# Output projection of a two-layer decoder trunk: half of its first-half products moved from attention to the projection stage

## The chip, the cores and the metric

The kernel runs on one core of a Trainium2 chip. TensorE (PE) multiplies, with its weight loads beside it (PEld); VectorE (DVE), ScalarE (ACT) and GpSimd (POOL) do elementwise work; SyncE (SP) issues all DMAs, in order. The metric is the device time of one execution in microseconds, as a median over runs.

## The reference

Two residual layers on x of 1024 tokens by 1024 features, float32. Layer 0 mixes with 8 forgetting-attention heads and 8 latent-attention (MLA) heads, layer 1 with 8 differential heads; both map the concatenated heads back by one output projection. A gated MLP with a causal convolution follows. What matters here:

```python
for layer in range(DEPTH):
    h = _rms_norm(x, norm_mix_pre[layer])
    m = mixer(h)                               # ends in: heads @ w_out
    x = x + _rms_norm(m, norm_mix_post[layer])
    h = _rms_norm(x, norm_ffn_pre[layer])
    f = _conv_ffn(h, ffn_w_up[layer], ...)
    x = x + _rms_norm(f, norm_ffn_post[layer])
```

## The kernel before, in words

Every float32 operand of a product is split into a high part, cast to the type float32r, and the low remainder; a product is three matmuls, high by high, high by low, low by high (mm3, L139). A split is a cast on ACT and a subtraction on POOL or DVE (L119).

Attention of a layer runs head by head as a generator. Beside it runs a second generator, "dense": the projections of later heads, and last out_first (L446), the first half of the output projection. weave (L286) takes steps of dense between the steps of a head, as much as a table entry for that head allows (MLA_DENSE L40, DIFF_DENSE L29, in units of 2400 columns, about a microsecond). A scheduler then sets each engine's order from dependences and its own estimate of times; each engine works its list in order.

The heads' outputs, transposed, go to DRAM as oT: 8 tiles of 128 features, in high and low parts. The output projection multiplies them, for each of 8 tiles of 128 tokens (m, from 7 down to 0), with w_out in two column halves of 512 (n). The features are taken in two groups of four, kg 0 and kg 1. In layer 0 group 0 are the forgetting heads and group 1 the MLA heads; in layer 1 group 0 are heads 0 to 3. So group 0 is ready while the later heads still run:

- out_first multiplies group 0 for both column halves, 8 x 2 x 12 = 192 matmuls per layer, and copies each sum on ACT (L459) to SBUF tiles opart.
- out_second (L462), after attention, multiplies group 1, again 192 matmuls, into a bank of tag S (n = 0) or mm (n = 1), adds opart on DVE (L479), and runs the two norms: fin_e after the first half (square on ACT L202, times gain on POOL L203), fin_a after the second (square L212, POOL's multiply L213, the row's scale by rstd_col L153, x updated on DVE L216 and L217, stored L219; then pre_norm_a: square L225, scale, xn L227). fin_b of the tile before transposes xn on PE (L235) and evacuates it as operands of the up-projection (ffn_in_evac L492; B, T1f, T2f, T4f).
- From tile 3 on the first two feature tiles of the up-projection are prepared (prep L551: weights wg, wv, their splits S3, S4, A11, A12, S1, S2, A22 in tiles of tag Q) and two of their products are run ahead (run_a L587).

Buffers with a part in this: Q 18 tiles of 128x512 (keys and queries of heads, then weights of the projection's first half, then prep's splits), WL 8 (loads of oT, named ot), X 14 quads, T 6 (x and xn of a token tile), raw 2, and in PSUM 2 banks of tag S and 2 of mm. In layer 1 a differential head ends in sub_a and sub_b (L1138, L1155): a square, a sum over features on PE (L1146), Newton steps on DVE, then the store to oT.

Of the kernel before, what the change touches and what calls it, by code (L numbers as in the profile page):

```python
# [19 lines left out]
P = 128  # L20
# [5 lines left out]
NP = 11  # L26
TAIL = 5
FOX_DENSE = (21, 21, 16, 16, 21, 21, 5, 13)
DIFF_DENSE = (29, 31, 28, 32, 30, 30, 28, 25)  # L29
GRAIN = 1  # L30
LAG = 8
NA = 2
# [4 lines left out]
VT = "Q"  # L37
SB = 4
P2T = "mm"
MLA_DENSE = (8, 8, 6, 6, 6, 7, 18, 18)  # L40
HALF = 512
EPS = 1e-6
BIG = 3.0e38
# [18 lines left out]
def trunk(ctx: ExitStack, tc: tile.TileContext, a: dict):  # L62
# [13 lines left out]
    def buf(tag, name):  # L76
        return sb.tile(SHAPE[tag], F32, tag=tag, name=nm(name), bufs=BUFS[tag])
# [3 lines left out]
    def bank(tag, n=HALF):  # L81
        return ps.tile([P, n], F32, tag=tag, name=nm("ps" + tag), bufs=PB[tag])
# [120 lines left out]
        nc.gpsimd.tensor_tensor(src, src, g_post[n], ALU.mult)  # L203
        return ss

    def post_late(m, n, src, sse, early, g_post, xi, xq, cut=False):


        xr, xn = xq
        cs, ce = (slice(i * HALF, (i + 1) * HALF) for i in (n, 1 - n))  # L210
        ss = small(1, "ssl")
        nc.scalar.activation(xn[:, cs], src, AF.Square, accum_out=ss)  # L212
        nc.gpsimd.tensor_tensor(src, src, g_post[n], ALU.mult)  # L213
        nc.vector.tensor_scalar(ss, ss, sse, None, ALU.add)
        r = rstd_col(ss, 1.0 / D, "post")
        nc.vector.scalar_tensor_tensor(xr[:, ce], early, r, xr[:, ce], ALU.mult, ALU.add)  # L216
        nc.vector.scalar_tensor_tensor(xr[:, cs], src, r, xr[:, cs], ALU.mult, ALU.add)  # L217
        for c in (ce, cs) if cut else (slice(0, D),):
            nc.sync.dma_start(xd[xi + 1][m * P:(m + 1) * P, c], xr[:, c])  # L219
# [210 lines left out]
                res.append((hi, lo))  # L430
        return res

    def oT_load(oT, kg, m):
        ts = []
        for j in range(2):
            t = buf("WL", "ot")
            nc.sync.dma_start(t.rearrange("p (k c) -> p k c", k=4),
                              oT[j, 4 * kg:4 * kg + 4, :, m * P:(m + 1) * P].rearrange("k p c -> p k c"))
            ts.append(t)
        return ts  # L440

    def wo_quads(w_src, k0, n):
        q = [buf("X", "wo") for _ in range(2)]
        return wo_load(w_src, k0, n, lambda k: (q[0][:, k, :], q[1][:, k, :]))

    def out_first(w_src, oT, part):  # L446

        w = [wo_quads(w_src, 0, n) for n in range(2)]
        for m in range(7, -1, -1):
            ot = oT_load(oT, 0, m)  # L450
            for n in range(2):
                if (m // 4, n) not in part:
                    part[m // 4, n] = buf("X", "opart")
                o = bank("mm")
                for k in range(4):
                    mm3(o, hl(tuple(t[:, k * P:(k + 1) * P] for t in ot), w[n][k]), k == 0, k == 3)
                    if k < 3:
                        yield
                nc.scalar.copy(part[m // 4, n][:, m % 4, :], o)  # L459
                yield  # L460

    def out_second(w_src, oT, part, fin_0, fin_e, fin_a, fin_b, ahead):  # L462


        w = [wo_load(w_src, 4, 0, lambda k: (buf("Q", "woh"), buf("Q", "wol"))), wo_quads(w_src, 4, 1)]
        ot = {m: oT_load(oT, 1, m) for m in (7, 6, 5)}
        fin_0(7)
        for m in range(7, -1, -1):
            if m >= 3:
                ot[m - 3] = oT_load(oT, 1, m - 3)  # L470
            if m:
                fin_0(m - 1)
            rows = []
            for n in range(2):
                o = bank("S" if n == 0 else "mm")
                r = part[m // 4, n][:, m % 4, :]
                for k in range(4):
                    mm3(o, hl(tuple(t[:, k * P:(k + 1) * P] for t in ot[m]), w[n][k]), k == 0, k == 3)
                nc.vector.tensor_tensor(r, r, o, ALU.add)  # L479
                rows.append(r)  # L480
                if n == 0:
                    fin_e(m, 0, r)
            fin_a(m, 1, rows[1], rows[0])
            if m < 7:
                fin_b(m + 1)
            if m == 3:
                ahead(0)
        ahead(1)
        fin_b(0)
# [551 lines left out]
    def mixer_end(layer, w_src, oT, part):  # L1041
        B, xqs, sse = {}, {}, {}
        gpost = gain_post(a["g_mix_post"][layer])
        gpre = gain_bc(a["g_ffn_pre"][layer], buf("T", "gain"))

        def fin_0(m):
            xqs[m] = xq_pair("T")
            x_load(m, 2 * layer, xqs[m])

        def fin_e(m, n, src):  # L1050
            sse[m] = post_early(n, src, gpost, xqs[m][1][:, :HALF])

        def fin_a(m, n, late, early):
            post_late(m, n, late, sse[m], early, gpost, 2 * layer, xqs[m])
            pre_norm_a(xqs[m], gpre)

        def fin_b(m):
            pre_norm_b(xqs.pop(m), ffn_in_evac(B, m))

        up = ffn_up(layer, B)  # L1060
        out_second(w_src, oT, part, fin_0, fin_e, fin_a, fin_b, lambda n: next(up))
        ffn_in_sums(B)
        run(up)
# [271 lines left out]
```

## Time and profile before

| | us |
|---|---|
| median of 3 runs (2611.28 to 2621.82) | 2616.64 |
| the profiled execution | 2621.89 |
| its span, first to last instruction | 2620.1 |
| layer 0: first product of out_second | 591.81 |
| layer 0: last xn of the stage starts | 674.20 |
| layer 1: first product of out_second | 1873.38 |

All times of an instruction are from the start of the span. The mean granted clock of TensorE was 0.971. Matmuls are pipelined: a row of n matmuls shows their first start to their last end, so the price of one is read from the start of the next row. A row of a group ends in its busy time, the mean in ns, and the idle time of the engine just before, with what ended it. A line number is that of the listing above; L142 is every product.

### The profile page before, as it was taken

The page shows a single profiled execution, that of the slowest core. Times are in us where ns is not written, and L with a number is a line of the kernel's source. Part 1 is how long each engine was busy: PE and PEld are TensorE (multiplying, and loading weights), DVE is VectorE, ACT ScalarE, POOL GpSimd, SP SyncE. Part 2 cuts the span into 40 slices and gives each one's busy share as a digit, 9 for nine tenths or more (in the row PEclk, how much of TensorE's full clock was granted, in tenths as well). Part 3 has the DMA queues.
Part 4 walks back from the last instruction along what each step waited for, and adds up shares of the span by engine and source line. Part 5 has one row for each costly group of instructions (what it writes and reads, how often), then busy time and mean ns, then how long its engine had stood idle before and what let it go on. Part 6 is the DMA issues. An engine that isn't in the chain of part 4 may idle for free. (4 is left out here: it accounts for less than half of the span.)

```text
span 2620.1 us, 36572 instructions
## 1 busy us (share of the span) xinstructions
PE 2467.1 (94%) x12326; PEld 2077.1 (79%) x12326; DVE 1768.7 (68%) x3631; ACT 1234.9 (47%) x2465; POOL 1299.1 (50%) x1172
## 2 busy tenths in 40 slices
PE   9999899998799999989989999999969999999897
PEld 7888688776688888878878888987757888887686
DVE  5555788657866666666665676777686666656768
ACT  4455578664433333434445555555454333334443
POOL 3445665435577677731321323322267777776132
PEclk9999999898899999999999999999989999999999
DMA  3332333335222323574542112133442332326545
GB/s 140 91 91 77 113 82 89 97 97 169 75 105 106 108 95 111 181 242 156 173 143 57 59 56 73 57 95 103 146 140 73 109 109 93 108 105 230 184 149 213
DMA packets 172156, 307.78 MB, mean 117 GB/s; under 512 B 16936, under 2 KB 67768, under 8 KB 171968
## 3 DMA queue, kind: packets, MB, share of 16 engines
q1 hardware_dynamic: 171968, 305.44, 35.7%
q8 instruction: 98, 1.61, 0.3%
q14 instruction: 90, 0.74, 0.1%
HBM read 213.84 MB, written 76.85 MB: 111 GB/s over the span
## 5 line engine op out<-in xcount | busy, mean ns | idle before, releaser
L142 PE MATMUL psmm<-hT,whi 128*128 128x512 f32 (+1 forms) x960 | 311.6, 401 | 0.6 <-DVE qb L315 0.5
L122 POOL TENSOR_TENSOR wlo<-wraw,whi 128x512 fp32r<-128x512 f32 (+2 forms) x96 | 130.5, 1367 | 266.4 <-ACT whi L121 241.3
L351 ACT ACTIVATE t<-t,mn 128x896 f32<-128x896 f32 (+7 forms) x256 | 198.9, 777 | 127.7 <-DVE mn L343 121.1
L142 PEld LDWEIGHTS psmm<-hT,whi 128*128 128x128 f32 (+1 forms) x960 | 176.1, 190 | 34.5 <-issue 0.7
L142 PE MATMUL psmm<-hT,wlo 128*128 128x512 f32 (+1 forms) x480 | 190.1, 397 | 0.0
L121 ACT CAST d<-uraw 128x512 fp32r<-128x512 f32 x154 | 91.6, 618 | 140.8 <-DMA uraw<-uS 82.6
L142 PE MATMUL psmm<-wo,ot 128*128 128x512 f32 x576 | 146.8, 397 | 0.0
L380 PE MATMUL pstr<-ident,t 128*128 128x128 f32 x864 | 136.4, 280 | 6.4 <-DVE t L1199 2.1
L122 POOL TENSOR_TENSOR d<-uraw,d 128x512 fp32r<-128x512 f32 x66 | 100.3, 1538 | 84.6 <-ACT d L121 83.7
L142 PE MATMUL psmm<-whi,hT 128*128 128x256 f32 (+1 forms) x576 | 123.0, 301 | 9.1 <-ACT hT L247 4.3
L122 DVE TENSOR_TENSOR d<-wdraw,d 128x512 fp32r<-128x512 f32 x88 | 88.4, 1026 | 58.4 <-ACT d L121 45.3
L142 PEld LDWEIGHTS psmm<-wo,ot 128*128 128x128 f32 x576 | 105.8, 189 | 20.7 <-DVE qb L315 0.2
L610 ACT ACTIVATE y<-gate,cols 128x1024 f32<-128x1024 f32 x44 | 50.8, 1155 | 147.9 <-DVE gate L605 147.9
L142 PE MATMUL pstr<-T,S3h 128*128 128x512 f32 x352 | 112.7, 401 | 5.1 <-DVE B L507 5.1
L142 PE MATMUL psmm<-B,A12h 128*128 128x512 f32 x352 | 110.9, 396 | 5.0 <-DVE B L507 5.0
L380 PEld LDWEIGHTS pstr<-ident,t 128*128 128x128 f32 x864 | 102.9, 145 | 15.9 <-POOL t L902 3.6
L122 DVE TENSOR_TENSOR S2l<-s,S2h 128x512 fp32r<-128x512 f32 x44 | 65.1, 1480 | 74.5 <-ACT S2h L121 74.5
L385 DVE TENSOR_TENSOR ptq<-pstr,ptq 128x512 fp32r<-128x512 f32 (+1 forms) x160 | 99.5, 630 | 23.6 <-ACT ptq L384 19.3
L614 ACT ACTIVATE y<-y,cols 128x1024 f32<-128x1024 f32 x44 | 50.7, 1153 | 135.9 <-DVE y L612 135.9
L603 DVE TENSOR_TENSOR u<-u,psmm 128x512 f32<-128x512 f32 x44 | 29.9, 680 | 117.9 <-PE psmm L142 117.9
L142 PE MATMUL psmm<-B,A11h 128*128 128x512 f32 x352 | 109.3, 390 | 0.0
L142 PE MATMUL psmm<-T,S2h 128*128 128x512 f32 x352 | 108.8, 390 | 0.0
(357 smaller groups left out, 7636.4 us busy)
## 6 DMA issues: line engine op xcount, KB each, us to landing
wdraw<-in_ffn_down_dram SPq DMA_DIRECT2D x60, 512.0 KB, 4.7
wg<-in_ffn_up_dram SPq DMA_DIRECT2D x44, 512.0 KB, 3.4
wv<-in_ffn_up_dram SPq DMA_DIRECT2D x44, 512.0 KB, 3.5
uS<-us SPq DMA_DIRECT2D x88, 256.0 KB, 2.0
uraw<-uS SPq DMA_DIRECT2D x40, 512.0 KB, 4.1
uA<-y SPq DMA_DIRECT2D x66, 256.0 KB, 2.1
ot<-oT SPq DMA_DIRECT2D x64, 256.0 KB, 3.5
uraw<-uA SPq DMA_DIRECT2D x30, 512.0 KB, 4.5
```

The lines of the kernel that those rows point to most:

```text
L121: nc.scalar.copy(R(hi), raw)
L122: lo_eng.tensor_tensor(R(lo), raw, hi, ALU.subtract)
L142: ins = nc.tensor.matmul(out, R(l), R(r), start=first and j == 0, stop=last and j == n - 1).ins
L351: nc.scalar.activation(t[:, :W], t[:, :W], AF.Exp, bias=mn, scale=-1.0, accum_out=l)
L380: nc.tensor.transpose(tp[:, c:c + P], pts[qi][:, b * P:(b + 1) * P], ident)
L385: nc.vector.tensor_tensor(R(pl[:, :c]), tp[:, :c], ph[:, :c], ALU.subtract)
L603: nc.vector.tensor_tensor(u2, s1, p6, ALU.add)
L610: nc.scalar.activation(y, gp, AF.Copy, scale=col(2, f))
L614: nc.scalar.activation(y, y, AF.Gelu_apprx_tanh, bias=cb)
```

## The change

out_first now multiplies group 0 only for the first column half. For the second half all eight feature tiles are summed in one bank of tag mm in out_second: group 1 first and group 0 behind it, but for token tile 7 group 0 first, which may be done before attention ends. The sum is not added to an opart. post_late squares it from PSUM, and instead of POOL's multiply in place, DVE multiplies it by the gain out of PSUM into the first half of that tile's xn (home), from where L217's line takes it. Weights of the second half's group 0 go to four Q tiles (high) and one X quad (low), and their oT loads to Q tiles. The tables of filler per head are smaller.

```diff
-DIFF_DENSE = (29, 31, 28, 32, 30, 30, 28, 25)
+DIFF_DENSE = (27, 29, 26, 30, 28, 27, 24, 20)
...
-MLA_DENSE = (8, 8, 6, 6, 6, 7, 18, 18)
+MLA_DENSE = (7, 7, 6, 5, 5, 6, 7, 7)
...
-    def post_late(m, n, src, sse, early, g_post, xi, xq, cut=False):
+    def post_late(m, n, src, sse, early, g_post, xi, xq, cut=False, home=None):
...
         nc.scalar.activation(xn[:, cs], src, AF.Square, accum_out=ss)
-        nc.gpsimd.tensor_tensor(src, src, g_post[n], ALU.mult)
+        if home is None:
+            nc.gpsimd.tensor_tensor(src, src, g_post[n], ALU.mult)
+        else:
+            nc.vector.tensor_tensor(home, src, g_post[n], ALU.mult)
+            src = home
...
-        w = [wo_quads(w_src, 0, n) for n in range(2)]
+        w = wo_quads(w_src, 0, 0)
         for m in range(7, -1, -1):
             ot = oT_load(oT, 0, m)
-            for n in range(2):
-                if (m // 4, n) not in part:
-                    part[m // 4, n] = buf("X", "opart")
-                o = bank("mm")
-                for k in range(4):
-                    mm3(o, hl(tuple(t[:, k * P:(k + 1) * P] for t in ot), w[n][k]), k == 0, k == 3)
-                    if k < 3:
-                        yield
-                nc.scalar.copy(part[m // 4, n][:, m % 4, :], o)
-                yield
+            if m // 4 not in part:
+                part[m // 4] = buf("X", "opart")
+            o = bank("mm")
+            for k in range(4):
+                mm3(o, hl(tuple(t[:, k * P:(k + 1) * P] for t in ot), w[k]), k == 0, k == 3)
+                if k < 3:
+                    yield
+            nc.scalar.copy(part[m // 4][:, m % 4, :], o)
+            yield
...
-        w = [wo_load(w_src, 4, 0, lambda k: (buf("Q", "woh"), buf("Q", "wol"))), wo_quads(w_src, 4, 1)]
+        lo = buf("X", "wo")
+        w1 = wo_load(w_src, 0, 1, lambda k: (buf("Q", "woh"), lo[:, k, :]))
+        o1 = {7: oT_load(oT, 0, 7, "Q")}
+        w0 = wo_load(w_src, 4, 0, lambda k: (buf("Q", "woh"), buf("Q", "wol")))
+        w1 += wo_quads(w_src, 4, 1)
         ot = {m: oT_load(oT, 1, m) for m in (7, 6, 5)}
+        o1[6] = oT_load(oT, 0, 6, "Q")
         fin_0(7)
         for m in range(7, -1, -1):
             if m >= 3:
                 ot[m - 3] = oT_load(oT, 1, m - 3)
+            if m < 7 and m:
+                o1[m - 1] = oT_load(oT, 0, m - 1, "Q")
             if m:
                 fin_0(m - 1)
             rows = []
             for n in range(2):
                 o = bank("S" if n == 0 else "mm")
-                r = part[m // 4, n][:, m % 4, :]
-                for k in range(4):
-                    mm3(o, hl(tuple(t[:, k * P:(k + 1) * P] for t in ot[m]), w[n][k]), k == 0, k == 3)
-                nc.vector.tensor_tensor(r, r, o, ALU.add)
+                ks = ((4, 5, 6, 7) if n == 0 else (0, 1, 2, 3, 4, 5, 6, 7) if m == 7 else (4, 5, 6, 7, 0, 1, 2, 3))
+                for k in ks:
+                    src = (ot if k > 3 else o1)[m]
+                    mm3(o, hl(tuple(t[:, (k % 4) * P:(k % 4 + 1) * P] for t in src), w0[k - 4] if n == 0 else w1[k]), k == ks[0], k == ks[-1])
+                if n == 0:
+                    r = part[m // 4][:, m % 4, :]
+                    nc.vector.tensor_tensor(r, r, o, ALU.add)
+                    fin_e(m, 0, r)
+                else:
+                    r = o
                 rows.append(r)
-                if n == 0:
-                    fin_e(m, 0, r)
...
-            post_late(m, n, late, sse[m], early, gpost, 2 * layer, xqs[m])
+            post_late(m, n, late, sse[m], early, gpost, 2 * layer, xqs[m], home=xqs[m][1][:, :HALF])
```

Three places show how the order of instructions moves. First PE in layer 1, in the last head, from the last product of the block that holds tokens 512 to 767 (pspv) to the sum of squares on it (pstr from ones; L1146 before, L1161 now) and the next transposes. Before, the end of 33 out_first products stands ahead of the sum:

```order
L142 MATMUL psmm_19694<-wo_18701,ot_19690 128x512
L142 MATMUL psmm_19694<-wo_18700,ot_19692 128x512
L1146 MATMUL pstr_19440<-ones,osh_19441 128x1 x2
L1146 MATMUL pstr_19440<-ones,osl_19445 128x1 x2
L380 MATMUL pstr_19472<-ident,t_19382 128x128
L380 MATMUL pstr_19472<-ident,t_19407 128x128
```

Now, at the same place, from the block's last product:

```order
L142 MATMUL pspv_19279<-ptq_13846,vd_17564 128x256 x3
L142 MATMUL pspv_19279<-ptq_13846,vd_17564 128x128 x3
L1161 MATMUL pstr_19392<-ones,osh_19393 128x1 x2
L1161 MATMUL pstr_19392<-ones,osl_19397 128x1 x2
L384 MATMUL pstr_19424<-ident,t_19341 128x128
L384 MATMUL pstr_19424<-ident,t_19366 128x128
```

The sum of squares follows the block's products directly; no product on wo stands between or behind it until out_second begins.

Second DVE in layer 0's stage, from tile 7's x update to the next tile's late half (opart_5538 and psS: first half; opart_5642 and psmm: second half; xr_7158 is tile 7). Before:

```order
L479 TENSOR_TENSOR opart_5538<-opart_5538,psS_7232 128x512
L160 TENSOR_SCALAR rrpost_7204<-cvpost_7203,rrpost_7204 128x1
L216 SCALAR_TENSOR_TENSOR xr_7158<-opart_5538,rrpost_7204,xr_7158 128x512
L217 SCALAR_TENSOR_TENSOR xr_7158<-opart_5642,rrpost_7204,xr_7158 128x512
L479 TENSOR_TENSOR opart_5642<-opart_5642,psmm_7249 128x512
L157 TENSOR_SCALAR cvpre_7216<-ss_7214 128x1
L214 TENSOR_SCALAR ssl_7263<-ssl_7263,sse_7246 128x1
L157 TENSOR_SCALAR cvpost_7267<-ssl_7263 128x1
L158 RECIPROCAL rrpre_7217<-cspre_7218 128x1
```

Now (xr_7055 and xn_7056 are tile 7, xn_7063 and psmm_7161 tile 6):

```order
L493 TENSOR_TENSOR opart_5631<-opart_5631,psS_7144 128x512
L220 SCALAR_TENSOR_TENSOR xr_7055<-opart_5631,rrpost_7112,xr_7055 128x512
L221 SCALAR_TENSOR_TENSOR xr_7055<-xn_7056,rrpost_7112,xr_7055 128x512
L157 TENSOR_SCALAR cvpre_7124<-ss_7122 128x1
L158 RECIPROCAL rrpre_7125<-cspre_7126 128x1
L159 TENSOR_SCALAR cvpre_7124<-cvpre_7124,rrpre_7125 128x1
L160 TENSOR_SCALAR rrpre_7125<-cvpre_7124,rrpre_7125 128x1
L231 SCALAR_TENSOR_TENSOR xn_7056<-xr_7055,rrpre_7125,gain_6982 128x1024
L216 TENSOR_TENSOR xn_7063<-psmm_7161,gain_6980 128x512
```

Before, tile 6's second half was taken (L479 on psmm) ahead of tile 7's second norm; now it is taken (L216) behind tile 7's xn.

Third SP in layer 0's stage, the last loads and stores (xr: x of a token tile; wg, wv: weights of the second feature tile of the up-projection). Before:

```order
L219 DMA xd_93<-xr_7315 128x1024
L197 DMA xr_7617<-in_x_dram 128x1024
L553 DMA wg_7852<-in_ffn_up_dram 128x1024
L219 DMA xd_93<-xr_7395 128x1024
L554 DMA wv_7853<-in_ffn_up_dram 128x1024
L197 DMA xr_7699<-in_x_dram 128x1024
```

Now (ot_7585 and ot_7587 are group 0 of token tile 1, ot_7682 and ot_7684 of tile 0):

```order
L197 DMA xr_7686<-in_x_dram 128x1024
L223 DMA xd_93<-xr_7432 128x1024
L568 DMA wg_7861<-in_ffn_up_dram 128x1024
L441 DMA ot_7585<-oT_100 128x4x128
L441 DMA ot_7587<-oT_100 128x4x128
L441 DMA ot_7682<-oT_100 128x4x128
L441 DMA ot_7684<-oT_100 128x4x128
L569 DMA wv_7862<-in_ffn_up_dram 128x1024
```

Four loads of group 0 now stand behind wg and ahead of wv.

More of the change, by code (lines that the diff above doesn't have):

```diff
@@ L431, in wo_load, with oT_load @@
         return res
-    def oT_load(oT, kg, m):
+    def oT_load(oT, kg, m, tag="WL"):
         ts = []
         for j in range(2):
-            t = buf("WL", "ot")
+            t = buf(tag, "ot")
             nc.sync.dma_start(t.rearrange("p (k c) -> p k c", k=4),
```

## The prediction

> **What bounds the kernel now.** I read the page's first part, then busy time by stretch, then what TensorE (PE) waits for in each output-projection stage, then single instructions there.
>
> ```profile
> PE 2467.1 (94%) x12326; PEld 2077.1 (79%) x12326; DVE 1768.7 (68%) x3631; ACT 1234.9 (47%) x2465; POOL 1299.1 (50%) x1172
> ```
>
> PE is the engine with least slack, but 94% is a mean over stages. The next rows part it (columns: stretch, its length, busy us of PE, PE's weight loads, DVE, ACT, POOL, each with its count, then granted clock).
>
> ```profile
> 505.00:586.00 81.00, 79.23 (x460) 68.26 (x458) 39.48 (x110) 47.22 (x107) 25.60 (x34) 1.00 0.28 80
> 591.80:642.00 50.20, 49.57 (x224) 40.85 (x224) 36.32 (x76) 24.58 (x58) 26.73 (x20) 0.95 0.55 177
> 642.00:679.00 37.00, 17.36 (x62) 12.90 (x63) 33.16 (x65) 16.14 (x40) 23.16 (x17) 0.68 0.32 112
> 1700.00:1853.00 153.00, 146.71 (x790) 123.98 (x790) 110.88 (x361) 84.89 (x193) 46.25 (x64) 0.97 0.35 105
> 1853.00:1874.00 21.00, 15.68 (x83) 12.87 (x83) 11.29 (x55) 6.49 (x16) 0.00 (x0) 0.90 0.42 134
> 1924.00:1960.00 36.00, 16.46 (x63) 12.49 (x64) 32.57 (x68) 16.96 (x41) 23.18 (x17) 0.72 0.34 118
> ```
>
> The last two MLA heads (505 to 586) hold PE busy 79.23 of 81 us with DVE at 39.48: PE alone bounds them, and this is where the old first half of the projection is filler. The last differential heads (1700 to 1853) are alike, 146.71 of 153. The second half of the projection goes the other way round: PE is full for 50 us, then has 17.36 of 37 us to do (16.46 of 36 in layer 1), while DVE is busy 33.16 of 37. So attention is PE's, and the end of the stage is DVE's. The waits of PE in layer 0's stage say the same:
>
> ```profile
> PE pstr L235 <- DVE xn L227: 11.1, 3, 7.1
> PE pspv L142 <- ACT B L506: 6.2, 1, 6.2
> PE psS L142 <- DMA ot<-oT: 5.2, 1, 5.2
> PE pstr L142 <- DVE B L507: 2.5, 1, 2.5
> ```
>
> About 20 us of PE (11.1 + 6.2 + 2.5) stand idle there behind DVE's norm chain, and 5.2 ahead of it for a load. The change moves matmuls from the stretch where PE is the bound into the one where it waits.
>
> **The change, part by part.** The price of a matmul and of eight transposes, from PE's instructions in order of time (start, duration, what):
>
> ```profile
> 602.26 2.88 PE L142 MATMUL psmm<-wo,ot 128*128 128x512 f32 x12
> 604.98 0.39 PE L142 MATMUL psS<-woh,ot 128*128 128x512 f32 x1
> ...
> 638.52 1.03 PE L235 MATMUL pstr<-ident,xn 128*128 128x128 f32 x8
> 639.31 2.07 PE L142 MATMUL psmm<-wo,ot 128*128 128x512 f32 x8
> ```
>
> Twelve take 604.98 - 602.26 = 2.72 us, so 0.227 each; eight transposes 0.79.
>
> *Out of attention, layer 0.* By the code 8 tiles x 4 features x 3 = 96 matmuls leave; 12 of token tile 7 are begun there anyway. 84 x 0.227 = 19.1 us. PE is 97.8% busy there, so 18.6; the last heads then run without filler for a somewhat longer piece, for which I take off 1.1: 17.5 us. The eight ACT copies that go lie beside PE work and count nothing; the tables of filler per head fall with the filler (their sums by 27 and 24) and have no price of their own.
>
> *Out of attention, layer 1.* Here the filler ran almost to the end:
>
> ```profile
> 1852.17 0.81 PE L142 MATMUL pspv<-ptq,vd 128*128 128x256 f32 x6
> 1852.81 5.03 PE L142 MATMUL psmm<-wo,ot 128*128 128x512 f32 x21
> 1857.68 0.50 PE L1146 MATMUL pstr<-ones,osh 128*128 128x1 f32 x4
> ...
> 1859.21 3.00 PE L142 MATMUL psmm<-wo,ot 128*128 128x512 f32 x12
> ...
> 1873.38 0.76 PE L142 MATMUL psS<-woh,ot 128*128 128x512 f32 x1 [2.73 <-DMA ot<-oT]
> ```
>
> And ACT's square, which the sum at 1857.68 reads:
>
> ```profile
> 1853.64 0.42 ACT L1144 ACTIVATE osh<-distq 128x256 f32<-128x256 f32 x1
> ```
>
> Of 192 matmuls 33 (21 + 12) lie behind 1852.81, so 159 ahead; afterwards all 108 (96 + 12) are ahead, by PE's order shown above. 51 x 0.227 x 0.96 = 11.1 us ahead. Behind it a chain runs (square, sum, Newton steps, store, load, first matmul), and only the 21 matmuls between the square's end at 1854.06 and 1857.68 delay it: 3.6 us. Together 14.7.
>
> Bounds of both: above, 19.1, every moved matmul won. Below, what this tail shows: of its 33 x 0.227 = 7.5 us only 3.6 were in the way, 48%; all 84 at that rate give 9.2. I take the upper rows, since the stretches with the filler are like 505 to 586 and not like the tail.
>
> *Into the stage.* PE has there 8 x 12 + 12 + 7 x 24 = 276 projection matmuls instead of 192: 62.7 us; the first up-projection products that PE's order puts among them, 24 x 0.227 = 5.4; transposes of seven tiles, 5.5. 73.6 us, so from 591.81 to 665.4, if nothing is waited for. Then tile 0's norm chain, which I read from tile 7's (DVE, ACT in order of time):
>
> ```profile
> 597.45 0.69 DVE L479 TENSOR_TENSOR opart<-opart,psS 128x512 f32<-128x512 f32 x1 [6.63 <-PE psS L142]
> 599.74 0.69 DVE L479 TENSOR_TENSOR opart<-opart,psmm 128x512 f32<-128x512 f32 x1 [1.60 <-PE psmm L142]
> ...
> 610.22 1.28 DVE L227 SCALAR_TENSOR_TENSOR xn<-xr,rrpre,gain 128x1024 f32<-128x1024 f32 x1
> ```
> ```profile
> 601.20 1.28 ACT L156 ACT_TABLE_LOAD   x1
> ```
> ```profile
> 674.20 2.39 DVE L227 SCALAR_TENSOR_TENSOR xn<-xr,rrpre,gain 128x1024 f32<-128x1024 f32 x1
> ```
>
> 599.74 to 611.50 is 11.8 us, 10.5 without the table load. 665.4 + 10.5 = 675.9, against 676.59 now. The extra 84 matmuls would cost nothing: they fill the 20 us.
>
> *DVE, ACT, POOL, per tile.* The add of the second half goes (0.677), a multiply by the gain out of PSUM comes (same engine, shape and source, so 0.677 too); POOL's multiply goes. From the groups of 591 to 680:
>
> ```profile
> L217 DVE SCALAR_TENSOR_TENSOR xr<-opart,rrpost,xr 128x512 f32<-128x512 f32 x8 | 10.1, 1261 | 0.0
> L216 DVE SCALAR_TENSOR_TENSOR xr<-opart,rrpost,xr 128x512 f32<-128x512 f32 x8 | 9.2, 1149 | 0.8 <-POOL opart L203 0.3
> L479 DVE TENSOR_TENSOR opart<-opart,psmm 128x512 f32<-128x512 f32 x8 | 5.4, 677 | 1.6 <-PE psmm L142 1.6
> ```
> ```profile
> L217 DVE SCALAR_TENSOR_TENSOR xr<-opart,rrpost,xr x8: 739/1246/1842, 604.8 to 668.6; 128x512 f32<-128x512 f32 x8
> ```
> ```profile
> L213 POOL TENSOR_TENSOR opart<-opart,gain 128x512 f32<-128x512 f32 x8 | 11.1, 1391 | 2.5 <-ACT xn L212 2.5
> ```
>
> I price DVE at no change. The trace lets one think of a small gain: the same xr line takes 739 ns at least and 1261 on average, 4.2 us over eight, and 11.1 us of POOL leave. (The Trainium skill, SBUF — State Buffer, "Who interferes with whom", says that a DVE instruction with two SBUF inputs contends with a GpSimd instruction that reads SBUF, and one with at most one does not; the flat 677 of the PSUM reads agrees. By that rule the stretch of xr shrinks in step with POOL's reads, an estimate of 1.7 us a layer, and the sum would be 3.4 us lower.) As ends I take 0 and 4.2 us per layer.
>
> *Order and loads.* Two things can lengthen the stage. DVE's order now finishes tile 7's xn before it multiplies tile 6, so the chain of one tile tends to follow that of another: at 9.1 us of PE per tile (36 x 0.227 + 0.79 + 0.1) a quiet chain just fits, as tile 7's 10.5 holds another tile's add and a stretched xr. And the new loads for tiles 1 and 0 stand in SP's queue behind the next up-projection weights, and reuse Q buffers that the projection's weights hold until tile 0's first half is done. Such a load lands so late after its issue:
>
> ```profile
> ot<-oT SPq DMA_DIRECT2D x64, 256.0 KB, 3.5
> ```
>
> PE has tile 0's other half to do meanwhile, 12 x 0.227 = 2.7 us. Together I take 2.5 us per layer; ends: -5 (0.7 from PE's sum, 4.2 from DVE) and +8 (3.5 for the load, 4.9 if eight chains of 10.5 replace 79.1 us on DVE from 597.45 to 676.59, less rounding). The other new instructions, 32 loads, are spread over 50 us in which the DMA share is 0.55; they cost nothing unless SP's queue holds one back, which is that case. The weights' second-half split moves nearer its use, ahead of the last scores; PE's own work covers it, and if Q came free late, it would show as a wait of a score on wo.
>
> **Sum.** -17.5 - 14.7 + 2 x 2.5 = -27.2 us. The profiled execution took 2621.89 (span 2620.1, 1.8 around it), 5 above the median 2616.64. So 2594.7 for that execution, 2589.4 at the median.
>
> **The rivals.** (a) *Attention gives back half.* The heads' softmax chains, without filler, leave PE idle as in 1853 to 1874 (15.68 of 21 busy). Then 2 x 9.2 are won: -18.4 + 5 = -13.4, 2603. For: that tail. Against: DVE at 39.48 of 81, so room for shorter heads.
>
> (b) *The late loads.* PE waits in both layers ahead of tile 1's second group: +8 each, -32.2 + 16 = -16, 2600. For: SP's order. (The Trainium skill, Perfetto Trace Analysis, "Optimization Strategy", holds that gaps that repeat on the engine that should be full can mean too few buffers for the next tile; no row of before shows it here.) Against: PE has 2.7 us of other work ready.
>
> (c) *The norm chains run one after another.* DVE in order, one tile's mult behind the other's xn. Now eight tiles take 79.1 us, 9.9 each. At tile 7's full 11.8 they take 94.4, +15.3 per layer: -32.2 + 30.6 = -1.6, 2615. From (79.1 + 22.7) / 8 = 12.7 us a tile on, the stage eats all of it and 13.1 us (0.5%, about what a measurement of this kernel can tell from none) more; at 13.5, with a stretched xr in each, +28.9 a layer, so 2642. For: DVE's new order. Against: 10.5 holds waits that other tiles filled.
>
> That nothing is moved is ruled out by the order: SP's rows above hold loads of the first features in the stage, and PE's rows of the tail no wo product.
>
> **How the numbers follow.** Forecast 0.60, all of it faster. (a) 0.16, half of it within 0.5%. (b) 0.10, 0.06 faster and 0.04 the same. (c) 0.14, 0.05 the same and 0.09 slower. So faster 0.74, same 0.17, slower 0.09. Lower end: twice 19.1 and 5 gives -48, and as all ends at once are unlikely I stop at -46, 2570; the upper end takes in (a), (b) and (c) to 11.7 us a tile: 2613. Outside lie about 0.11 above and 0.06 below.
>
> **What would show it.** Right: the stage's first product on woh (591.81 and 1873.38 now) starts 17.5 us earlier in layer 0 and 17.5 - 2.5 + 14.7 = 29.7 earlier in layer 1; PE is nearly full from there for 70 us; its waits on xn and B shrink from 20 to some 10 us; the last xn ends about 87 us behind that start. Wrong: idle PE in the last heads waiting for mn, t or ptq (a); a PE wait on ot in mid-stage (b); DVE idle on ssl, cspost and cvpre in every tile and over 11 us from mult to mult (c).

## The result, and the profile after

| | runs | median, us | lowest to highest | profiled execution: time, span |
|---|---|---|---|---|
| before | 5 | 2621.82 | 2611.28 to 2625.39 | 2621.89, 2620.1 |
| changed | 5 | 2590.97 | 2587.53 to 2596.06 | 2590.97, 2589.2 |

The ratio is 0.9892, 95% interval 0.9876 to 0.9909: the changed kernel is faster, by 28.3 us of 2620 by the ratio, by 30.9 us between these medians and by as much between the two spans. The prediction was 2589.4.

The page's first part, of the changed kernel:

```profile
PE 2461.4 (95%) x12326; PEld 2073.5 (80%) x12326; DVE 1761.4 (68%) x3631; ACT 1229.2 (47%) x2449; POOL 1274.3 (49%) x1156
```

Over the whole program little is to be seen. By stretch (the same columns as in the prediction's table: length, then busy us of PE, PE's weight loads, DVE, ACT, POOL, then granted clock, DMA share, GB/s), layer 0:

```profile
500.00:550.00 50.00, 48.68 (x284) 41.61 (x283) 28.20 (x82) 31.14 (x70) 20.52 (x22) 1.00 0.34 99
550.00:570.10 20.10, 10.61 (x72) 8.66 (x70) 10.51 (x25) 10.52 (x27) 7.80 (x11) 0.82 0.91 288
570.10:645.50 75.40, 75.22 (x348) 62.21 (x348) 55.19 (x114) 34.10 (x81) 33.87 (x23) 0.98 0.57 183
645.50:692.00 46.50, 34.26 (x137) 27.65 (x138) 35.56 (x49) 20.28 (x35) 24.90 (x15) 0.82 0.15 51
```

PE is now busy 75.22 of the stage's first 75.40 us, as forecast ("nearly full from there for 70 us"). The second row is the other side of it: at the end of attention PE stands idle 9.5 of 20.1 us, and the granted clock is 0.82. Before, the 20.1 us ahead of the stage had 7.0 us of idle time and a clock of 0.95:

```profile
571.70:591.80 20.10, 13.09 (x96) 11.55 (x96) 12.22 (x38) 13.06 (x32) 7.57 (x11) 0.95 0.49 152
```

What PE waits for in the changed kernel between 500 and 700 us (line, what it waits for: us, times, longest):

```profile
PE pstr L239 <- DVE xn L231: 6.4, 1, 6.4
PE psS L142 <- DMA ot<-oT: 6.4, 1, 6.4
PE pstr L142 <- DVE B L522: 3.8, 1, 3.8
PE psmm L142 <- DVE B L522: 2.1, 1, 2.1
```

In the same window before had, beside the rows in the prediction, one more wait on B:

```profile
PE psmm L142 <- DVE B L507: 2.5, 1, 2.5
```

So the waits on xn and B have gone from 22.3 to 12.3 us, and all that are left lie behind the stage's last product. The wait for ot ahead of the first product stays: 5.2 before, 6.4 now.

For an account by steps I use instructions that both programs have once: the stage's first product on woh, the first activation of the feed-forward, the first cast of hT in the next layer. These rows are before's, as far as the prediction does not show them, then the changed kernel's:

```profile
591.81 0.77 PE L142 MATMUL psS<-woh,ot 128*128 128x512 f32 x1 [5.19 <-DMA ot<-oT]
708.46 1.15 ACT L614 ACTIVATE y<-y,cols 128x1024 f32<-128x1024 f32 x1
1326.36 0.58 ACT L247 CAST hT<-pstr 128x512 fp32r<-128x512 f32 x1
```
```profile
570.19 0.77 PE L142 MATMUL psS<-woh,ot 128*128 128x512 f32 x1 [6.37 <-DMA ot<-oT]
691.80 1.15 ACT L629 ACTIVATE y<-y,cols 128x1024 f32<-128x1024 f32 x1
1308.72 0.58 ACT L251 CAST hT<-pstr 128x512 fp32r<-128x512 f32 x1
1843.16 0.79 PE L142 MATMUL psS<-woh,ot 128*128 128x512 f32 x1 [2.31 <-DMA ot<-oT]
```

With the feed-forward's first activation of layer 1 at 1989.34 before and 1960.65 after:

| step | before, us | after, us | difference | forecast |
|---|---|---|---|---|
| layer 0 up to its stage | 591.81 | 570.19 | -21.6 | -17.5 |
| stage 0, to the first activation | 116.65 | 121.61 | +5.0 | +2.5 |
| feed-forward 0 | 617.90 | 616.92 | -1.0 | 0 |
| layer 1 up to its stage | 547.02 | 534.44 | -12.6 | -14.7 |
| stage 1, to the first activation | 115.96 | 117.49 | +1.5 | +2.5 |
| the rest | 630.76 | 628.55 | -2.2 | 0 |

Each is one execution. How far such a row can be trusted shows where other kernels of this study run the same instructions: the changed kernel's code of layer 0 up to its stage was profiled three times more, with the stage starting at 573.78, 572.54 and 569.84 (runs layer0_only, diff_old and pool_gain), and before's once more, at 590.27 (layer1_only). So a step is uncertain by 2 to 3 us, and by the means of these the first step is -19.5 and not -21.6.

### The profile page after: what moved, and what is told of

The parts are those of the page before. It is cut to its first block, busy times and chain, and to the rows that moved or that the text cites. A ratio compares the mean times of both kernels' runs of the same rounds, so it can differ in the third digit from the quotient of the medians.

```text
span 2589.2 us, 36629 instructions
## 1 busy us (share of the span) xinstructions
PE 2461.4 (95%) x12326; PEld 2073.5 (80%) x12326; DVE 1761.4 (68%) x3631; ACT 1229.2 (47%) x2449; POOL 1274.3 (49%) x1156
## 4 chain that ended last, share of the span: by engine, by line
PE 49%; DVE 13%; POOL 9%; DMA 7%; issue 5%; ACT 4%; SPq 0%; DVEq 0%; POOLq 0%; ACTq 0%
PE psmm L142 23%; PE psS L142 10%; PE pspv L142 7%; PE pstr L142 6%; DVE d L122 2%; PE pstr L384 2%; DMA wv<-in_ffn_up_dram 2%; POOL s L583 1%; DMA wdraw<-in_ffn_down_dram 1%; POOL s L579 1%; DMA uraw<-uA 1%; POOL A12l L122 1%; DVE wdraw L699 1%; POOL d L122 1%; DVE t L347 1%
## 5 line engine op out<-in xcount | busy, mean ns | idle before, releaser
L142 PE MATMUL psmm<-wo,ot 128*128 128x512 f32 x448 | 123.7, 396 | 0.0
L142 PE MATMUL pstr<-T,A22h 128*128 128x512 f32 x352 | 108.7, 389 | 0.0
L142 PEld LDWEIGHTS psmm<-hT,wlo 128*128 128x128 f32 (+1 forms) x480 | 90.9, 189 | 21.1 <-POOL wlo L122 1.0
L122 DVE TENSOR_TENSOR S2l<-s,S2h 128x512 fp32r<-128x512 f32 x44 | 57.0, 1295 | 74.2 <-ACT S2h L121 74.2
```

The lines of the kernel that those rows point to most:

```text
L122: lo_eng.tensor_tensor(R(lo), raw, hi, ALU.subtract)
L142: ins = nc.tensor.matmul(out, R(l), R(r), start=first and j == 0, stop=last and j == n - 1).ins
```

## The experiments

All ratios are to the kernel before on the same chip; "against changed" is the difference of a ratio to 0.9892, times 2620 us, uncertain by about 6 us, since each ratio is by 0.0016.

| run | median, us | ratio and interval | against changed |
|---|---|---|---|
| left_out | 2575.31 | 0.9831 [0.9814, 0.9849] | -16 |
| defer_more | 2605.10 | 0.9945 [0.9930, 0.9960] | +14 |
| tiles76_in_wait | 2582.77 | 0.9859 [0.9837, 0.9880] | -9 |
| pool_gain | 2592.44 | 0.9899 [0.9881, 0.9917] | +2 |
| layer0_only | 2602.71 | 0.9944 [0.9929, 0.9958] | |
| layer1_only | 2606.62 | 0.9952 [0.9940, 0.9964] | |
| old_tables | 2604.03 | 0.9940 [0.9927, 0.9953] | +13 |
| new_tables | 2605.40 | 0.9952 [0.9939, 0.9965] | |
| mla_old | 2595.16 | 0.9904 [0.9889, 0.9919] | +3 |
| diff_old | 2600.21 | 0.9930 [0.9916, 0.9944] | +10 |
| last_entries | 2612.44 | 0.9968 [0.9958, 0.9978] | |
| early_split | 2598.95 | 0.9923 [0.9908, 0.9938] | +8 |

The first theory was the prediction's: the moved matmuls are won in attention, where PE is the bound, and mostly hidden in the stage, where it waited. Its rivals: the stage has become PE's and pays for them in full, or DVE's chains pace it. The tables were taken to be without a price.

**Are the matmuls hidden in the stage? left_out.** The products are not made at all, their loads stay:

```diff
-                ks = ((4, 5, 6, 7) if n == 0 else (0, 1, 2, 3, 4, 5, 6, 7) if m == 7 else (4, 5, 6, 7, 0, 1, 2, 3))
+                ks = (4, 5, 6, 7)
```

> This kernel leaves out the products of the second column half with the first four feature tiles altogether (192 matmuls in both layers; that half of the projection is not computed in full); their loads stay. Theory (the moved matmuls are hidden in the stages): 24 of them, token tile 7's, leave heads in which PE is full, 24 x 0.227 = 5.4 us; the other 168 leave the stages, which the two traces show only 4.9 and 1.5 us longer than before up to the first activation of the feed-forward. So at most 11.8 us less than the changed kernel's 2591: about 2579, 2573 to 2587. Rival (PE has become the bound of the stage, each matmul costs its price): 192 x 0.227 = 43.6 less, 2547.

Measured 2575.3, inside the theory's range. Its stage 0 opens with two products on wo, at 570.30, and takes 112.5 us from there to the first activation (682.76) against 121.6 in the changed kernel; stage 1 takes 114.4 (1832.08 to 1946.48) against 117.5. So 84 matmuls, 19.1 us by price, are worth 9.1 us in one stage and 3.1 in the other, each by 2 to 3: some half and some five sixths are hidden. In this trace the feed-forward behind stage 0 takes 4.9 us more than in the changed kernel (621.79 against 616.92), so that only 4.2 us are left at the next attention; why was not looked into. Without the 84 matmuls PE waits for the norm chain again (of left_out, 565 to 683 us):

```profile
PE pstr L239 <- DVE xn L231: 14.1, 3, 11.9
```

**Is there room for more? defer_more.** In the first column half too, tiles 3 to 0 are done in the stage, the weights being kept:

```diff
-        for m in range(7, -1, -1):
-            ot = oT_load(oT, 0, m)
+        for m in range(7, 3, -1):
+            ot = oT_load(oT, 0, m)
...
-                ks = ((4, 5, 6, 7) if n == 0 else
+                ks = ((4, 5, 6, 7) if n == 0 and m > 3 else (4, 5, 6, 7, 0, 1, 2, 3) if n == 0 else
...
+                    if m > 3:
                         nc.vector.tensor_tensor(r, r, o, ALU.add)
+                    else:
+                        nc.vector.tensor_copy(r, o)
```

> Of the first column half too, token tiles 3 to 0 take all eight feature tiles in the stage: 48 more matmuls a layer leave attention, 10.9 us by price. Theory (PE is nearly full in the stage now, 77.2 us of 84.9 in the changed kernel's layer 0, the rest being waits at its end that nothing fills): what attention wins, 2 x 10.6, the stage gives back, 2 x 10.9: 2591, no change against the changed kernel, 2586 to 2598. Rival (DVE's norm chains still bound the stage and PE has room): another 10 to 20 us less, 2571 to 2581.

Measured 2605.1, 14 us slower than the changed kernel: the rival falls, and the theory was too kind. Attention won 8.9 and 6.0 us (stage 0 at 561.28; layer 1 528.5 us up to its stage against 534.4) where 10.6 each was expected, and the stages gave back 11.5 and 15.8 (133.1 and 133.3 us) where 10.9 was. From the stage's start to its last xn PE is busy 92.34 us with DVE at 68.08:

```profile
561.28:663.50 102.22, 92.34 (x411) 75.23 (x412) 68.08 (x141) 40.88 (x96) 35.97 (x27) 0.92 0.46 150
```

So with these tables 48 matmuls more cost 14 us. Two things stay open. The tables were not fitted to the smaller filler, which in layer 1 now ends 51.7 us ahead of the stage instead of 26.9, so a part of the loss may be theirs. And no run moves fewer matmuls, so where the best number lies is not shown. Why stage 1 gave back 5 us above the price was not looked into.

**Does DVE pace the stage? pool_gain.** The gain goes back to POOL, behind a copy by ACT:

```diff
-            nc.vector.tensor_tensor(home, src, g_post[n], ALU.mult)
+            nc.scalar.copy(home, src)
+            nc.gpsimd.tensor_tensor(home, home, g_post[n], ALU.mult)
```

> The multiply by the gain goes back to POOL: ACT copies the bank to SBUF, POOL multiplies in place; DVE loses eight multiplies a layer (5.4 us). Theory (PE paces the stage, DVE has some slack, and only the last tile's chain lies on the path): the chain is longer by ACT's copy and 0.7 us (1.39 against 0.68), some 1.3 us a layer, and the xr and xn lines read SBUF beside POOL again, up to 1.7 a layer: 2 to 6 us slower than the changed kernel, 2593 to 2597. Rival (DVE is the bound of the stage): 5.4 us less on DVE in each layer, 4 to 10 us faster, 2581 to 2587.

Measured 2592.4, 2 us above the changed kernel and no difference that the interval can tell; the rival's 4 to 10 us faster is not seen. The groups of DVE in layer 0's stage, of the changed kernel (570 to 657 us) and of pool_gain (569 to 657; operation, out<-in, count, then busy us and mean ns):

```profile
L220 DVE SCALAR_TENSOR_TENSOR xr<-opart,rrpost,xr 128x512 f32<-128x512 f32 x8 | 7.0, 879 | 0.5
L221 DVE SCALAR_TENSOR_TENSOR xr<-xn,rrpost,xr 128x512 f32<-128x512 f32 x8 | 6.0, 746 | 0.0
L216 DVE TENSOR_TENSOR xn<-psmm,gain 128x512 f32<-128x512 f32 x8 | 5.5, 683 | 3.7 <-ACT xn L212 3.7
```
```profile
L221 DVE SCALAR_TENSOR_TENSOR xr<-opart,rrpost,xr 128x512 f32<-128x512 f32 x8 | 8.8, 1096 | 0.5
L222 DVE SCALAR_TENSOR_TENSOR xr<-xn,rrpost,xr 128x512 f32<-128x512 f32 x8 | 6.6, 827 | 1.2 <-POOL xn L217 1.2
```

The xr lines took 19.3 us before (10.1 + 9.2), take 13.0 now, and 15.4 with POOL's multiply back, while the multiply out of PSUM costs 683 ns, near the 677 that the prediction gave it. But the third line of DVE that reads two tiles of SBUF goes the other way (the changed kernel, then pool_gain):

```profile
L231 DVE SCALAR_TENSOR_TENSOR xn<-xr,rrpre,gain 128x1024 f32<-128x1024 f32 x8 | 13.6, 1696 | 0.1
```
```profile
L232 DVE SCALAR_TENSOR_TENSOR xn<-xr,rrpre,gain 128x1024 f32<-128x1024 f32 x8 | 11.6, 1455 | 0.1
```

Over the three lines it is 31.9 us before, 26.6 now and 27.0 with POOL's multiply back in layer 0, and 29.9, 26.6 and 29.4 in layer 1. (The Trainium skill, SBUF — State Buffer, "Who interferes with whom", has the rule that the prediction's estimate of 1.7 us a layer went by. Layer 1's sums agree with its direction; in layer 0 the 5.3 us that went did not come back with POOL's multiply, so there the rule is not shown to be the cause.) The time hardly moved either way.

**Do the layers add up? layer0_only, layer1_only.** One layer keeps the code and table of before:

```diff
-        out_second(w_src, oT, part, fin_0, fin_e, fin_a, fin_b, lambda n: next(up))
+        (out_second_b if layer == 1 else out_second)(w_src, oT, part, fin_0, fin_e, fin_a, fin_b, lambda n: next(up))
```

(and `layer == 0` in the other; out_first alike.)

> The change in layer 0 alone (layer 1 with the code and the table of before). By the two traces' landmarks layer 0 gave 21.6 us before its stage and the stage gave 4.9 back, 17.7 us in all up to the next attention: 2604 where before is 2622. The prediction's terms give 15.0: 2607. Rival (the surplus of 21.6 over the price of 84 matmuls, 19.1, is an accident of one execution): 13 to 15, 2607 to 2609.

> The change in layer 1 alone. By the landmarks 12.6 us in attention, 1.5 given back in the stage, and 2.2 behind it that nothing explains: 11 to 13 us under before, 2609 to 2611; the prediction's terms give 12.2. Rival (layer 1 depends on what layer 0 had moved: the two do not add up): under 8, or over 16.

By the ratios layer 0 gives 14.7 us and layer 1 12.6, in all 27.3 of 28.3: they add up. In layer 0 that is the prediction's 15.0 and its rival's 13 to 15, so the 17.7 of the landmarks was in part an accident of one execution. The profiled execution of layer0_only was its slowest, 2612.28, so its trace is used only for the spread above.

**Have the tables no price? old_tables, new_tables.** The changed code with the two old tables, and the old code with the new ones:

```diff
-MLA_DENSE = (7, 7, 6, 5, 5, 6, 7, 7)
+MLA_DENSE = (8, 8, 6, 6, 6, 7, 18, 18)
-DIFF_DENSE = (27, 29, 26, 30, 28, 27, 24, 20)
+DIFF_DENSE = (29, 31, 28, 32, 30, 30, 28, 25)
```

> The changed kernel with the old tables of filler per head. Theory (the tables have no price of their own, they only follow the filler; with the old ones it runs out in the last heads, which then wait for their softmax): 0 to 6 us slower than the changed kernel, 2591 to 2597, and no filler in the last head. Rival (the 3.3 us wait of PE on ptq at 478 us, and the low clock behind it, went because of the tables): the wait is back, 4 to 5 us slower, with that row in the trace.

> The kernel before with the new tables: the same filler, less of it beside each head, the rest alone behind the last head. Theory (the heads are bound by PE, so filler taken out of them shortens them as much as it costs behind them, but for waits that come up): 0 to 8 us slower than before, 2622 to 2630. Rival (the tables are where the gain comes from): 5 to 30 us faster, 2592 to 2617.

Both expectations of the theory fall, and so does the first rival: with the old tables PE has no wait above 0.3 us from 470 to 500 us, so the wait on ptq went for another reason. The new tables alone make the old code 13 us faster, and without them the changed code loses 13 of its 28. The moved products, with what goes with them, are then worth 15.7 us with either pair of tables (0.9940 with the old ones, 0.9892 against 0.9952 with the new ones). The rows say how. The end of layer 0's attention with the old code and new tables, then the end of layer 1's with old code and new tables, with changed code and old tables, and with both changed:

```profile
540.00:582.27 42.27, 42.27 (x255) 37.03 (x254) 21.80 (x63) 27.58 (x64) 16.70 (x21) 1.00 0.41 124
1808.00:1858.89 50.89, 48.06 (x279) 41.86 (x278) 29.98 (x108) 25.67 (x61) 9.47 (x14) 1.00 0.40 130
```
```profile
1808.00:1854.65 46.65, 32.71 (x164) 28.11 (x163) 33.12 (x118) 20.82 (x51) 10.82 (x14) 0.71 0.54 161
```
```profile
1808.00:1843.16 35.16, 25.75 (x133) 21.47 (x133) 25.06 (x101) 16.21 (x43) 9.38 (x14) 0.80 0.63 209
```
```profile
PE pstr L1179 <- POOL osh L1176: 6.8, 2, 5.9
```

In the old code smaller entries leave filler for the end of the last head and for the time in which its output is stored and loaded again; PE is full there, and the wait for ot is gone in layer 0 and 0.6 us in layer 1. With the old table the changed code's filler has run out at 1813 us, 42 us ahead of the stage, the last head waits 5.9 us for POOL's osh (the last row), and the granted clock is 0.71. With the new one the filler ends 27 us ahead, the longest such wait is 1.5 us, and the clock is 0.80. So a second theory: a table acts by what it leaves for the end of the last head. Its rival: it acts evenly, through all entries.

**Where do the tables act? mla_old, diff_old, last_entries.** One old table in the changed kernel (the lines above, one at a time), and in the kernel before only the two last entries:

```diff
-MLA_DENSE = (8, 8, 6, 6, 6, 7, 18, 18)
+MLA_DENSE = (8, 8, 6, 6, 6, 7, 7, 7)
```

> The changed kernel with the old table in layer 0 alone. The run with both old tables was some 13 us slower than the changed kernel. Theory (a table matters by what filler it leaves for the end of the last head, where PE otherwise waits; in layer 0 the filler is used up by 540 us with either table): little of the 13, 0 to 4 us slower than the changed kernel, so ratio 0.989 to 0.991. Rival (the tables work evenly on both layers): half of it, 6 to 7 us, ratio 0.9915 to 0.992.

> The changed kernel with the old table in layer 1 alone. Theory (with the old one the filler is used up at about 1810 us, some 45 us ahead of the stage, with the new one about 25 us ahead; the last head then waits 5.9 us for POOL's osh and runs at a granted clock of 0.71): most of the 13, 7 to 12 us slower than the changed kernel, ratio 0.992 to 0.994. Rival (evenly): 6 to 7 us; rival (the tables do nothing in layer 1, the difference was in layer 0): ratio 0.989.

> The kernel before with only the last two entries of layer 0's table changed, from 18 to 7. Theory (these leave filler behind the last head, which covers the 5.2 us wait for ot and keeps the clock up): most of what the new table gave in layer 0, where its trace is 9.5 us ahead at the stage and 6.7 at the feed-forward: 5 to 9 us faster than before, ratio 0.9965 to 0.998, and no wait on ot ahead of the first product of the stage. Rival (the table acts through all its entries): 0 to 3 us, ratio 0.999 or more.

All three came out as the second theory had it: 3 us of the 13 in layer 0, 10 in layer 1, and two entries alone bring the old code 8 us (0.9968). There PE's wait for ot, between 500 and 590 us, is 0.2 us in place of 5.2:

```profile
PE psS L142 <- DMA ot<-oT: 0.2, 1, 0.2
```

That the two layers differ is clear, since no execution of diff_old was as fast as the slowest of mla_old; the sizes 3 and 10 are each uncertain by 6 us. In layer 0 of the old code the last entries are shown to do it. In layer 1 all entries were changed at once, so that it is the last ones there is argued from the rows and not shown.

**Have the weights' splits no price? early_split.** In before's trace PE stands still once in the middle of layer 0's attention. DVE, PE and the stretch behind (columns as above):

```profile
476.88 3.19 DVE L122 TENSOR_TENSOR wo<-woraw,wo 128x512 fp32r<-128x512 f32 x2
480.60 0.67 DVE L385 TENSOR_TENSOR ptq<-pstr,ptq 128x512 fp32r<-128x512 f32 x1
481.32 1.01 PE L142 MATMUL pspv<-ptq,Vm 128*128 128x256 f32 x3 [3.25 <-DVE ptq L385]
480.00:490.00 10.00, 8.68 (x41) 8.20 (x42) 6.71 (x20) 4.79 (x13) 4.17 (x7) 0.66 0.33 96
```

Two splits of the second half's weights stand on DVE ahead of the ptq that PE needs; PE waits 3.25 us and then runs at 0.66. The changed kernel splits these weights from 498 us on, never two in a row on DVE, and its clock from 480 to 490 is 1.00:

```profile
480.00:490.00 10.00, 9.66 (x63) 8.19 (x63) 8.86 (x27) 7.53 (x17) 3.29 (x4) 1.00 0.34 91
```

The experiment puts them back where they were:

```diff
+        part["w1"] = wo_quads(w_src, 0, 1)
...
-        lo = buf("X", "wo")
-        w1 = wo_load(w_src, 0, 1, lambda k: (buf("Q", "woh"), lo[:, k, :]))
+        w1 = part["w1"]
```

> The changed kernel, but the second column half's weights of the first four features are loaded and split where the kernel before did it, at the start of the filler; everything else as changed. Theory (in before two such splits on DVE, 3.2 us, stand ahead of ptq at 477 us, PE waits 3.3 us and runs at a granted clock of 0.66 behind it; moving them nearer their use won this): 3 to 6 us slower in layer 0, in both layers 3 to 10 us slower than the changed kernel, ratio 0.9905 to 0.993, and the wait on ptq is back. Rival (the splits are hidden wherever they stand): no change, ratio 0.989.

Measured 2599.0, 8 us slower than the changed kernel. The stall is back, put down to DVE's next product oso and not to ptq:

```profile
477.14 3.44 DVE L122 TENSOR_TENSOR wo<-woraw,wo 128x512 fp32r<-128x512 f32 x2
481.19 1.64 PE L142 MATMUL pspv<-ptq,Vm 128*128 128x256 f32 x4 [3.24 <-DVE oso L412]
480.00:490.00 10.00, 8.73 (x41) 8.10 (x42) 7.09 (x19) 4.91 (x14) 4.72 (x9) 0.66 0.48 144
```

Its stage 0 starts at 579.41, 11.6 us ahead of before's mean of 591.0 where the changed kernel's mean is 19.5 ahead. So some 8 us of layer 0's gain come from where the splits stand, and the 84 matmuls alone win about 11.6 (one trace, by 2 to 3). Layer 1 shows nothing of it: 531.2 us up to its stage, where the changed code takes 528.6 to 534.4. So the cost is one stall, not a price of each split.

The changed kernel still has such a place. The first half's weights are split as a pair too, and PE waits behind it for mn, which DVE makes next; before has the same wait, of 2.72 us. No run moves this pair:

```profile
461.50 3.33 DVE L122 TENSOR_TENSOR wo<-woraw,wo 128x512 fp32r<-128x512 f32 x2
465.61 0.55 PE L142 MATMUL psS<-mq,mq 96*128 96x128 f32 x3 [2.71 <-DVE mn L347]
```

**A version faster than both: tiles76_in_wait.** The products of tiles 7 and 6 with the first features are tied behind attention's last product, so that they run while PE waits for ot:

```diff
-... if m == 7 else (4, 5, 6, 7, 0, 1, 2, 3))
+... if m > 5 else (4, 5, 6, 7, 0, 1, 2, 3))
+                if n == 1 and m in (7, 6):
+                    pace["after"] = pace["end"]
...
+    pace["end"] = pace["last"]
     run(dense)
     mixer_end(0, a["e_out"], oT_d[0], part)
```

> The first-feature products of token tiles 7 and 6 are held until the last product of attention and run before the first load of the last features lands, where PE waited 6.4 us in layer 0 and 2.3 in layer 1. Theory (PE paces heads and stage): in layer 0 24 x 0.227 = 5.4 less, in layer 1 2.3 less: 7.7 under the changed kernel, 2583. Rival 1 (the norm chain of DVE paces the stage from tile 7 on, so only what leaves the heads counts): 12 x 0.227 = 2.7 in each layer at most, 2586 to 2588. Rival 2 (the loads of tile 6 land late): no gain, 2591 or more.

Measured 2582.8, 9 us under the changed kernel by the ratios, near the theory's 7.7, though rival 1's 2586 to 2588 lies inside what these ratios leave open. By layer its trace (an execution of 2587.59) bears out neither. The rows of PE at the place in layer 0 (start, duration, what):

```profile
563.60 0.44 PE L142 MATMUL psmm<-woh,ot 128*128 128x512 f32 x1
...
568.88 0.39 PE L142 MATMUL psmm<-woh,ot 128*128 128x512 f32 x1
569.11 0.39 PE L142 MATMUL psS<-woh,ot 128*128 128x512 f32 x1
...
571.38 0.73 PE L142 MATMUL psS<-woh,ot 128*128 128x512 f32 x2 [1.20 <-DMA ot<-oT]
```

24 matmuls fill 563.60 to 569.11, the wait for ot is 1.2 us, and the clock from 540 to 569 us is 1.00 where it was 0.89. Stage 0 then takes 114.2 us to the first activation instead of 121.6, and the next attention starts 8.4 us earlier, more than the theory's 5.4. In layer 1 the theory's 2.3 is not seen: from the start of attention to the first activation that trace takes 653.3 us against 651.9. The wait for ot is gone there too, but ten of the 24 run at 0.43 us each, and all of them stand ahead of the last head's sum of squares, whose square is done at 1830.42:

```profile
1829.35 0.73 PE L142 MATMUL psmm<-woh,ot 128*128 128x512 f32 x1
...
1836.54 0.50 PE L1164 MATMUL pstr<-ones,osh 128*128 128x1 f32 x4
```

So the total came out by one layer alone; that the late sum is what spoils the other is not shown.

## Why the prediction was right, and where it was not

The total was right to 2 us (2589.4 against 2591.0), and the gain of 27.2 us is near the 28.3 of the ratio and the 30.9 of the medians. That is in part luck: two steps were wrong with opposite signs, and 2589.4 starts from a median of 2616.64, which five runs put at 2621.82. Its steps:

- **Matmuls out of layer 0's attention, -17.5.** Measured -21.6 in the profiled execution, -19.5 by the means. The size is near and the working is not: 84 matmuls "at 97.8%" win some 11.6, between the two ends given (9.2 and 19.1) and nearer the lower. "A somewhat longer piece, for which I take off 1.1" was mis-sized; it is nearer 7. Rival (a), idle PE, is the smaller part of it. From the start to the stage PE's busy time and matmuls are, in before, early_split and the changed kernel:

```profile
0.00:591.81 591.81, 556.71 (x3135) 476.89 (x3135) 382.45 (x1075) 359.65 (x793) 285.88 (x370) 0.98 0.33 98
0.00:579.41 579.41, 542.01 (x3051) 463.80 (x3051) 381.44 (x1075) 355.78 (x785) 287.53 (x370) 0.97 0.36 106
0.00:570.19 570.19, 534.10 (x3050) 456.90 (x3051) 380.61 (x1075) 355.10 (x785) 287.72 (x370) 0.98 0.36 106
```

  With 84 matmuls fewer (early_split) PE is busy 14.7 us less, not 19.1, and idle 2.3 us more: from 540 us to the stage its granted clock is 0.91, where before has 0.98. In the changed kernel the idle time of the whole layer is within 1 us of before's, 36.1 against 35.1.
- **"PE's own work covers" the weights' splits.** Failed, to the good: they were not covered where they stood before. Moving them won some 8 us, which hid the miss above.
- **The tables "fall with the filler" and "have no price of their own".** Failed. The 96 matmuls that leave a layer are 20.5 of the tables' units (96 x 512 / 2400), and the tables fell by 27 and 24, so they also shift what is left towards the stage. This carries 13 us of the 28, 3 in layer 0 and 10 in layer 1 by the ratios. In the changed kernel's layer 1 the filler now ends 27 us ahead of the stage and not 42; in layer 0 it ends 34 to 38 us ahead with either table, and there the table does little.
- **Layer 1's attention, -14.7.** Measured -12.6 here; in the four kernels with the change and the new table in layer 1 (the changed one, mla_old, layer1_only, pool_gain) it lasts 534.4, 530.2, 530.5 and 528.6 us, on the mean 16.1 less than the 547.0 of before. With the old table (diff_old, old_tables) it lasts 536.2 and 539.4, 9.2 less. So the size came out, but the matmuls alone win 9.2 and not 11.1 + 3.6, and about 7 are owed to the table, which the sum put at nothing.
- **The stages, +2.5 each.** Measured +5.0 and +1.5, inside the ends of -5 and +8. PE is full as forecast, and the waits left are 12.3 us ("some 10"). The last xn ends 84.9 and 85.6 us behind the stage's start (forecast 87; before 84.8 in both), so what the order and the late loads were to cost up to there is hardly seen. The extra in layer 0 lies behind it, where the sum had no term: 31.9 us from the last xn's end to the activation before, 36.8 after. The prediction followed the chain of tile 0 alone, but PE waits 6.4 us for the xn of tile 1, which starts 75.0 us behind the stage's start before and 80.3 after; the up-projection's products that need it start 3.9 us ahead of the last xn's end before and 2.5 us behind it after. In layer 1 that xn is late by as much (75.0 and 81.0) and only 1.5 us came of it, so this is not shown to be all of it.
- **DVE at no change.** Right in its effect, as far as pool_gain can tell.
- **Rival (b), the late loads.** Ahead of the stage PE waits for ot as before; in mid-stage only this, between 500 and 700 us, so it falls. This is the row:

```profile
PE psmm L142 <- DMA ot<-oT: 0.3, 1, 0.3
```

- **Rival (c), the chains in series.** The multiplies L216 of tiles 7 and 0 start at 578.96 and 646.77, 67.8 us for seven steps, 9.7 each, at PE's pace and under the 11 us that would have spoken for (c). With 48 matmuls more (defer_more) the stage eats the gain, with PE busy 92 us to the last xn and DVE 68.

## What to carry to other kernels

Work that fills one engine beside a chain was worth most here at the chain's end, where store, load and the last softmax leave the engine idle: look at the last 20 us ahead of each stage before counting moved matmuls at full price, and set the filler so that it lasts until there. A table that was fitted to the old code is part of the change: run the old code with the new table too, which here took 13 of the 28 us. When a change moves a product, look at what goes with it, its weights' loads and splits: in layer 0 their place was worth some 8 us beside the 12 of the products themselves. A sum that comes out right can hold two errors of opposite sign, and only runs that undo one part at a time show them.

## What the runs showed of the hardware

**A wait cost more than its length.** After the 6.4 us wait for ot the changed kernel's first matmuls of the stage take about 0.43 us each instead of 0.227, for some 3 us:

```profile
570.76 0.63 PE L142 MATMUL psS<-wol,ot 128*128 128x512 f32 x1
571.18 1.05 PE L142 MATMUL psmm<-wo,ot 128*128 128x512 f32 x2
572.04 1.05 PE L142 MATMUL psS<-woh,ot 128*128 128x512 f32 x2
573.19 0.62 PE L142 MATMUL psS<-woh,ot 128*128 128x512 f32 x2
```

The two that start at 571.18 last until the next at 572.04, 0.86 us; twelve at full clock took 2.72 in before, 0.45 for two. The wait of 3.25 us in before was followed by a granted clock of 0.66 over 10 us. (The Trainium skill, TensorE: Matmul & The Clock Gate, "Why this matters for your kernels", warns of gaps over about 3 us, after which the clock is halved; the 0.43 against 0.227 agrees.) Filling the gap won both in layer 0 of tiles76_in_wait: there the matmuls behind it take 0.23 us from the third on.

**Two splits at once.** A split on DVE takes 0.67 to 0.69 us at the least; two in a row take 3.19 and 3.44 where POOL splits at the same time, about 1.6 to 1.7 each. In the two single cases at hand the later of the two engines was slowed: in the changed kernel a split of DVE at 528.74, 0.09 us ahead of one on POOL, keeps its 0.69 us, and POOL's takes 1.73 in place of 1.28; in before one of DVE at 547.02, 0.48 us behind POOL's, takes 1.37. The stall of early_split stands behind such a pair.
